# Feed-forwards tied to the written plan: layer 0's whole, layer 1's up to its part-sum products

## The chip, the cores and the metric

The kernel runs on one core of one Trainium2 chip. The metric is the device time of one execution in microseconds (us); for several runs the median is given. A core has TensorE (PE; its weight loads are PEld in the profile), VectorE (DVE), ScalarE (ACT), GpSimd (POOL) and SyncE (SP), whose instruction streams run side by side and wait for each other through semaphores. All bulk transfers of this kernel are issued from SP's queue.

## The reference, cut to what matters

Two layers over 512 latent tokens and 256 context tokens of width 1024, in 32-bit floating point. Each layer is a token mixer (windowed attention in layer 0, differential attention in layer 1) and a feed-forward of width 4096, each followed by a residual and a LayerNorm. Layer 1 needs only the latent tokens.

```python
alpha = DEEPNORM_ALPHA                                   # (2 * DEPTH) ** 0.25
x = layer_norm(alpha * x + g1 * ax, ln1_g[i], ln1_b[i])
fx = sqrelu_mlp(x * (1.0 + sc2) + sh2, mlp_w1[i], mlp_w2[i])
x = layer_norm(alpha * x + g2 * fx, ln2_g[i], ln2_b[i])
...
def sqrelu_mlp(h, w1, w2):
    return jnp.square(jax.nn.relu(h @ w1)) @ w2
```

g1, g2, sc2 and sh2 are vectors over the width that come from a conditioning product; g1 and g2 are called gates below.

## The kernel before, in words

**Products.** Every large product is three matmuls of split operands (`mm3`, L330 to L332): a value is cast to a shorter format (the "h" part, on ACT) and what the cast lost is a second number (the "l" part, a subtraction on DVE). `wsplit` (L305) loads 128 x 1024 of a weight and does that cast (L313) and split (L319). A weight buffer of the pool has three raw tiles and four h/l pairs.

**A feed-forward.** `main0` and `main1` begin with the attention's output product by blocks of 128 tokens (`tok_product`, tile `y_ps`): six blocks in layer 0, four in layer 1. Behind each block stands a chain: `gated_add` (L586) multiplies the product by the gate row (`g_tmp`, L589) and adds it to the block's accumulator `acc`; `stats` takes its statistics (`bn`); `moments` makes mean and 1/deviation (`mv`, `rstd`, the power on POOL); `normalise` (L538) scales the block in place (L540). Then `ln_job` (L544) has TensorE transpose the block (`xn_t`, L555), ACT apply the scale and shift (`fx` or `hx_v`) and cast (`hx0m`, `hx1m`, `hx`), and DVE split. The residual for the second LayerNorm is needed from the same block: `residual` (L685) multiplies `acc` by the first LayerNorm's weight row and adds its bias row; both rows were multiplied by alpha before (`scale_inplace`, L699). In layer 0, `R0.step` runs it and sends the block to `m_spill`.

`mlp_pipe` (L702) computes the first six column tiles of w1 plainly (`plain`, tile `h_ps`) and the other 26 as 13 pairs with seven instead of eight half products (`pair`; the weights' sums are made by `part_sums`, on POOL, ACT and DVE). Between them run pieces of the second product (`y_groups`, tile `y_ps`, collected in `fx`). At the end `last_y` multiplies what was collected by the second gate and adds it to `acc` (`fold`, two POOL operations for each half block, 24 in layer 0), then runs the last products and the chain of the next LayerNorm behind each block (`final`, L956). In layer 0, `pre1` then starts layer 1's first products (`qkv_ps`).

**The order.** The kernel's code contains a planner, `Flow`. Jobs are generators that yield what they wait for; the planner keeps a time `T` for TensorE, gives every DVE (D), ACT (A), POOL (G) and DMA (Q) operation a price (`dve`, `act`, `pool2`: 0.60, 0.50 and 1.25 us for 512 elements a partition; a DMA of 1024 1.45 us and 2 us to land) and a latency (0.2 us, for the end of `normalise` LNLAT = 6.0, for the last block of layer 0 2.5), and so decides in which order the jobs emit their TensorE work. TensorE's queue is in that order. An operation starts in the plan when its engine is free and its dependencies are done; where several could, the one with the lowest number (the order of making). An operation without dependencies may start earlier in the plan than the time at which it was emitted.

The other engines' queues are ordered by the framework's own list scheduler. Where `fl.pin` is "DAG", each DVE, ACT and POOL operation that has a dependency in the plan gets an order edge from the one before it on its engine, so that the queue is as planned; where it is "", no edges are made. Before the change it is "DAG" from layer 0's attention (L1203), "" from layer 0's feed-forward (L1476), "DAG" in layer 1's attention (L1631) and "" in layer 1's feed-forward (L1973). Most planned operations appear in the profile under the lines of their helpers: DVE L267, ACT L270, POOL L273, DMAs L279; a DVE operation that is also tied behind a certain matmul has L678.

## Time and profile before

| what | value |
|---|---|
| median of 3 runs | 1643.1 us (1641.33 to 1644.98) |
| the profiled execution's own time | 1639.2 us |
| its span, first to last instruction | 1637.4 us |
| mean granted clock of TensorE | 0.991 |
| layer 0's feed-forward | about 308 to 892 us |
| layer 1's feed-forward | about 1250 us to the end |

The profile is one execution, taken by the hardware's profiler. Its page gives busy times and shares by engine; a group line gives an operation by source line, engine, tiles and shape, how often it ran, its busy time and the mean time of one in ns, and then the idle time of its engine just before it with what ended that idle time. A wait line reads: engine and line, what it waited for, total us, times, longest us. A timeline row reads: start, length, engine, line, operation, output<-inputs, shape, how many were merged, and in brackets the idle time before it and what ended it. A windows row gives busy time and instructions of an engine in a stretch, then the clock that TensorE was granted (1.00 is full), the DMA share and the rate. What is named as the end of a wait is inferred; "issue" means that the profile shows nothing.

### The profile page before, as it was taken

How to read it: one execution, taken by the hardware profiler on the slowest of the kernel's cores; microseconds unless marked ns; L12 is line 12 of the kernel's file. 1: busy time of each engine (PE TensorE's matmuls, PEld its weight loads, DVE VectorE, ACT ScalarE, POOL GpSimd, SP SyncE). 2: the span in 40 equal slices, each digit the busy share in tenths (PEclk: the TensorE clock that was granted, in tenths of full speed). 3: DMA queues.
4: the chain of work that ended last, by engine and by line, in shares of the span. 5: the costliest groups of instructions: out<-in, count | busy, mean ns of one | idle time of the engine just before them, and what ended most of it. 6: DMA issues, size and time to landing. Idle time of an engine off the chain costs nothing.

```text
span 1637.4 us, 25213 instructions
## 1 busy us (share of the span) xinstructions
PE 1571.6 (96%) x9465; PEld 1377.9 (84%) x9465; DVE 1142.4 (70%) x2201; ACT 791.2 (48%) x1679; POOL 433.7 (26%) x369
## 2 busy tenths in 40 slices
PE   7999999989999999999997999999999799999998
PEld 5887677779888888888986999999987788888896
DVE  4655676589686777967576677777765876566667
ACT  3465665365334334333425555556552745544450
POOL 1344453102111211121183122220100123223363
PEclk9999999999999999999998999999999899999999
DMA  9111551533344444444332222211132333333321
GB/s 372 48 53 34 181 175 44 173 118 129 102 146 163 142 132 139 158 139 148 110 133 91 81 71 71 72 49 40 39 107 100 104 116 103 103 103 103 103 68 62
DMA packets 66435, 181.18 MB, mean 111 GB/s; under 512 B 7368, under 2 KB 13320, under 8 KB 66312
## 3 DMA queue, kind: packets, MB, share of 16 engines
q1 hardware_dynamic: 66312, 179.56, 32.6%
q8 instruction: 74, 1.21, 0.3%
q14 instruction: 49, 0.40, 0.1%
HBM read 168.49 MB, written 11.04 MB: 110 GB/s over the span
## 4 chain that ended last, share of the span: by engine, by line
PE 78%; DVE 9%; ACT 5%; POOL 3%; issue 3%; DMA 2%; SPq 0%; DVEq 0%; ACTq 0%; POOLq 0%
PE y_ps L331 9%; PE y_ps L332 9%; PE y_ps L330 9%; PE h_ps L330 7%; PE h_ps L331 7%; PE h_ps L332 7%; PE qkv_ps L330 3%; PE qkv_ps L331 3%; PE qkv_ps L332 3%; PE s_ps L1785 2%; PE o_ps L1395 2%; PE pT_ps L1413 2%; PE o_ps L1823 2%; POOL acc L273 1%; PE q_ps L330 1%
## 5 line engine op out<-in xcount | busy, mean ns | idle before, releaser
L331 PE MATMUL y_ps<-w_l,hid 128*128 128x512 f32 (+1 forms) x648 | 255.0, 393 | 1.6 <-DVE w_l L319 1.6
L330 PE MATMUL y_ps<-w_h,hid 128*128 128x512 f32 (+1 forms) x648 | 255.7, 395 | 0.6 <-DVE fx L267 0.6
L332 PE MATMUL y_ps<-w_h,hid 128*128 128x512 f32 (+1 forms) x648 | 254.9, 393 | 0.0
L319 DVE TENSOR_TENSOR w_l<-w_raw,w_h 128x1024 fp32r<-128x1024 f32 (+1 forms) x133 | 160.1, 1212 | 47.9 <-ACT w_h L313 46.4
L313 ACT CAST w_h<-w_raw 128x1024 fp32r<-128x1024 f32 (+1 forms) x133 | 131.1, 1002 | 104.8 <-PE y_ps L332 76.7
L332 PEld LDWEIGHTS y_ps<-w_h,hid 128*128 128x128 f32 x648 | 122.2, 189 | 28.6
L331 PEld LDWEIGHTS y_ps<-w_l,hid 128*128 128x128 f32 x648 | 122.3, 189 | 27.5 <-DVE w_l L319 2.9
L267 DVE TENSOR_TENSOR w_half<-w_raw,w_half 128x512 fp32r<-128x512 f32 x130 | 105.8, 824 | 54.7 <-ACT w_half L270 54.3
L330 PEld LDWEIGHTS y_ps<-w_h,hid 128*128 128x128 f32 x648 | 122.4, 189 | 25.4 <-DVE fx L267 1.0
L270 ACT CAST w_half<-w_raw 128x512 fp32r<-128x512 f32 x130 | 79.2, 621 | 128.0 <-PE h_ps L332 97.8
L330 PE MATMUL qkv_ps<-w_h,hx 128*128 128x384 f32 (+1 forms) x384 | 128.6, 335 | 3.2 <-ACT w_h L313 3.2
L273 POOL TENSOR_TENSOR w_sum<-w_raw 128x512 f32<-128x512 f32 x26 | 42.7, 1643 | 328.0 <-DMA w_raw<-in_w 265.1
L331 PE MATMUL qkv_ps<-w_l,hx 128*128 128x384 f32 (+1 forms) x384 | 123.6, 322 | 2.5 <-DVE w_l L319 2.5
L273 POOL TENSOR_TENSOR e<-e,sm 128x512 f32<-128x512 f32 (+2 forms) x96 | 93.5, 990 | 112.7 <-DVE sm L267 77.8
L332 PE MATMUL qkv_ps<-w_h,hx 128*128 128x384 f32 (+1 forms) x384 | 122.9, 320 | 0.0
L267 DVE TENSOR_TENSOR fx<-y_ps,fx 128x512 f32<-128x512 f32 x110 | 75.2, 686 | 36.1 <-PE y_ps L332 35.8
L270 ACT ACTIVATE relu<-relu 128x384 f32<-128x384 f32 (+3 forms) x104 | 69.3, 671 | 61.2 <-DVE relu L267 59.9
L273 POOL TENSOR_TENSOR rope<-rope,rope 128x256 f32<-128x256 f32 (+1 forms) x40 | 35.3, 883 | 216.3 <-DVE rope L267 138.8
L273 POOL TENSOR_TENSOR w_raw<-w_raw,w_sum 128x512 f32<-128x512 f32 x26 | 39.1, 1506 | 197.3 <-DVE w_half L267 160.4
L678 DVE CUSTOM_DVE_ANT_0 w_raw<-w_raw,cB 128x512 f32<-128x512 f32 x112 | 84.0, 784 | 4.7 <-PE y_ps L332 4.1
L270 ACT ACTIVATE e<-e,nm 128x513 f32<-128x513 f32 (+2 forms) x96 | 65.9, 687 | 30.8 <-DVE nm L267 26.8
L330 PEld LDWEIGHTS qkv_ps<-w_h,hx 128*128 128x128 f32 x384 | 72.8, 189 | 5.7 <-ACT w_h L313 3.6
(268 smaller groups left out, 4315.1 us busy)
## 6 DMA issues: line engine op xcount, KB each, us to landing
w_raw<-in_w SPq DMA_DIRECT2D x128, 512.0 KB, 3.6
w_raw<-in_w_adaT SPq DMA_DIRECT2D x56, 512.0 KB, 3.8
w_raw<-in_w_ada SPq DMA_DIRECT2D x24, 512.0 KB, 4.0
w_raw<-in_b_w SPq DMA_DIRECT2D x32, 384.0 KB, 3.9
raw<-in_w_ada SPq DMA_DIRECT2D x16, 512.0 KB, 9.6
w_raw<-in_a_wq SPq DMA_DIRECT2D x8, 512.0 KB, 8.7
w_raw<-in_a_wo SPq DMA_DIRECT2D x8, 512.0 KB, 4.2
w_raw<-in_b_wo SPq DMA_DIRECT2D x8, 512.0 KB, 4.5
```

Source lines behind the costliest of these rows:

```text
L267: return fl.op("D", dve(n), deps, lat, fn(**kw))
L270: return fl.op("A", act(n), deps, lat, fn(**kw))
L273: return fl.op("G", us, deps, lat, fn(**kw))
L313: last["cast"] = nc.scalar.copy(out=h[:, :n], in_=raw[:, :n])
L319: last["split"] = nc.vector.tensor_tensor(**kw)
L330: nc.tensor.matmul(out=o, lhsT=lh, rhs=rh, start=start, stop=False, **kw)
L331: nc.tensor.matmul(out=o, lhsT=lh, rhs=rl, start=False, stop=False, **kw)
L332: last["pe"] = nc.tensor.matmul(out=o, lhsT=ll, rhs=rh, start=False, stop=stop, **kw)
L678: i = fn(**kw)
L1395: nc.tensor.matmul(out=po[odd * HD:odd * HD + HD, 0:256], lhsT=vv[:, kb, kvh], rhs=pt_[:, odd * 256:odd * 256 + 256], start=(i == 0), stop ...
L1413: nc.tensor.transpose(out=pp[:, c * P:(c + 1) * P], in_=es[j][:, i * P:(i + 1) * P], identity=ident)
L1785: nc.tensor.matmul(out=sp[:, c * 512:c * 512 + 384], lhsT=qTt[:, tt, hl, qb * P:(qb + 1) * P], rhs=kS[:, tt, c * 384:c * 384 + 384], start ...
```

## The change

- Both feed-forwards begin with `fl.pin = "DAG"`; the chain of order edges isn't restarted before layer 1's attention. In layer 1 the pin is set to "" after the plain products, where the part sums begin. In layer 0 the pin stays, but from that place on `fl.loose` leaves the casts and splits of weights (in `wsplit` and in `part_sums`) without edges.
- LNLAT goes from 6.0 to 0.2, for the last block of layer 0 too.
- `residual` takes the unscaled rows and multiplies by alpha itself: two `scalar_tensor_tensor` in place of two `tensor_tensor`. The scalings of the rows (two in layer 0, two in layer 1) are gone. In the plan the residual now depends on the rows' transfers and, in layer 0, on TensorE's place.
- `fl.low` adds LOW = 100 to an operation's number: for layer 0's residuals and for the first two tiles of w1.
- `w1` asks for a w1 tile once, one tile ahead; the first two of layer 0 when the fifth block's chain is emitted, the first of layer 1 at the third block's. Layer 0's first three transfers get an order edge behind the last transfer of gate rows and accumulators.
- The final adds depend in the plan on the folds of their half block; `done` gets the statistics of both halves (`flat` resolves such nested lists).

```diff
-LNLAT = 6.0
+LNLAT = 0.2
+LOW = 100
@@ Flow.op
-        t.eng, t.us, t.seq = eng, us, self.n
-        for d in deps:
+        t.eng, t.us, t.seq = eng, us, self.n + LOW * self.low
+        for d in flat(deps):
@@ wsplit
-        a = fl.op("A", act(n), [q, hg], ins=last["cast"])
+        a = fl.op("A", act(n), [q, hg], ins=None if fl.loose else last["cast"])
...
-            d = fl.op("D", dve(n), [a], ins=last["split"])
+            d = fl.op("D", dve(n), [a], ins=None if fl.loose else last["split"])
@@ reload
-        dma(D - c0, [], out=b[:, c0:], in_=src[:, c0:].broadcast_to([P, D - c0]))
+        return dma(D - c0, [fl.pe(0.0)], out=b[:, c0:], in_=src[:, c0:].broadcast_to([P, D - c0]))
@@ residual
-    def residual(acc, g, b, after=None):
-        d = dv(D, [], behind(nc.vector.tensor_tensor, after), out=acc, in0=acc, in1=g, op=ALU.mult)
-        return dv(D, [d], nc.vector.tensor_tensor, out=acc, in0=acc, in1=b, op=ALU.add)
+    def residual(acc, g, b, deps, after=None):
+        d = dv(D, deps, behind(nc.vector.scalar_tensor_tensor, after), out=acc, in0=acc, scalar=ALPHA, in1=g, op0=ALU.mult,
+               op1=ALU.mult)
+        return dv(D, [d], nc.vector.scalar_tensor_tensor, out=acc, in0=b, scalar=ALPHA, in1=acc, op0=ALU.mult, op1=ALU.add)
@@ before mlp_pipe
+    W1 = {}
+
+    def w1(l, ft):
+        if ft < 6 and (l, ft) not in W1:
+            kept = queue["behind"]
+            if l == 0 and ft < 3:
+                queue["behind"] = queue["w1"]
+            W1[l, ft] = wsplit(t["w1"][l, ft])
+            queue["behind"] = kept
+        return W1.get((l, ft))
@@ plain
+                        W[ft] = w1(l, ft)
+                        w1(l, ft + 1)
...
-                        W[ft] = wsplit(t["w1"][l, ft])
@@ last_y, final
-                              half == 1 if l else half == 0 or tb == ntb - 1)
+                              half == 1 if l else half == 0 or tb == ntb - 1, more=[folds[half, tb]])
@@ mlp_pipe, after the plain products
+        if l == 0:
+            fl.loose = True
+        else:
+            fl.pin = ""
         weights(3, 4)
@@ layer 0's feed-forward
-    fl.pin = ""
+    fl.pin = "DAG"
...
+        queue["w1"] = queue["last"]
...
         def done1(tb, st, r):
+            if tb == NTB - 2:
+                fl.low = True
+                w1(0, 0)
+                w1(0, 1)
+                fl.low = False
...
-                d = residual(acc[tb], gx, gc, last["pe"])
+                fl.low = True
+                d = residual(acc[tb], gx, gc, rows + [fl.pe(0.0)], last["pe"])
+                fl.low = False
...
-            for b_, i in ((gx, 0), (gc, 1)):
-                reload(b_, lnrow[0, i:i + 1])
-                scale_inplace(b_, ALPHA)
+            rows[:] = [reload(b_, lnrow[0, i:i + 1]) for b_, i in ((gx, 0), (gc, 1))]
...
-                          LNLAT if tb < NTB - 1 else 2.5), 0)
+                          LNLAT), 0)
@@ layer 1's attention
-        fl.prev, fl.pin = {}, "DAG"
+        fl.loose = False
+        fl.pin = "DAG"
@@ layer 1's feed-forward
-    fl.pin = ""
+    fl.pin = "DAG"
...
-        scale_inplace(lb, ALPHA)
...
         def done3(tb, st, r):
+            if tb == NXB - 2:
+                w1(1, 0)
...
-            reload(gx, lnrow[1, 0:1])
-            scale_inplace(gx, ALPHA)
-            res = [lambda tb=tb: residual(acc[tb], gx, lb, last["pe"]) for tb in range(NXB)]
+            row = reload(gx, lnrow[1, 0:1])
+            res = [lambda tb=tb: residual(acc[tb], gx, lb, [row], last["pe"]) for tb in range(NXB)]
```

More of the change, by code (lines that the diff above doesn't have):

```diff
@@ L60, in __init__, with flat @@
         self.done, self.ins = None, None
+def flat(x):
+    return [z for y in x for z in flat(y)] if isinstance(x, (list, tuple)) else [x]
 class Flow:
@@ L74, in __init__ @@
         self.events = []
-        self.prev, self.order, self.pin = {}, None, ""
+        self.prev, self.order, self.pin, self.loose, self.low = {}, None, "", False, False
     def pe(self, us):
@@ L583, in hxs, with gated_add @@
         return hx[k // 2][:, k % 2, hl, sl]
-    def gated_add(pool, give, acc, half, pt, p, gate, last, scale=1.0):
+    def gated_add(pool, give, acc, half, pt, p, gate, last, scale=1.0, more=()):
         cs_ = slice(half * 512, (half + 1) * 512)
@@ L596, in gated_add @@
                       op0=ALU.mult, op1=ALU.add)
+        m = [m, *more]
         if last:
-            return dv(512, [m], nc.vector.tensor_tensor, out=acc[:, cs_], in0=acc[:, cs_], in1=tm, op=ALU.add)
-        return gp(pool2(512), [m], nc.gpsimd.tensor_tensor, out=acc[:, cs_], in0=acc[:, cs_], in1=tm, op=ALU.add)
+            return dv(512, m, nc.vector.tensor_tensor, out=acc[:, cs_], in0=acc[:, cs_], in1=tm, op=ALU.add)
+        return gp(pool2(512), m, nc.gpsimd.tensor_tensor, out=acc[:, cs_], in0=acc[:, cs_], in1=tm, op=ALU.add)
     def tok_mm(src, W, tb, pt, u):
@@ L752, in half @@
                 w = R.half_tile(nhalf[0] - 1)
-                a = ac(512, [dep, R.rhalf.get()], nc.scalar.copy, out=w[:, 0:512], in_=src)
-                d = dv(512, [a], nc.vector.tensor_tensor, out=w[:, 512:1024], in0=src, in1=f(w)[:, 0:512],
-                       op=ALU.subtract)
+                a = nc.scalar.copy(out=w[:, 0:512], in_=src)
+                a = fl.op("A", act(512), [dep, R.rhalf.get()], ins=None if fl.loose else a)
+                d = nc.vector.tensor_tensor(out=w[:, 512:1024], in0=src, in1=f(w)[:, 0:512], op=ALU.subtract)
+                d = fl.op("D", dve(512), [a], ins=None if fl.loose else d)
                 rel = Task()
@@ L895, in pair @@
             yield from mix(3)
-        gates, st, Wy, fresh = [], {}, {}, set()
+        gates, st, Wy, fresh, folds = [], {}, {}, set(), {}
         def y_weights(c, half, n=2):
@@ L920, in fold @@
             d = gp(pool2(512), [d], nc.gpsimd.tensor_tensor, out=x, in0=x, in1=g[:, cs_], op=ALU.mult)
-            gp(pool2(512), [d], nc.gpsimd.tensor_tensor, out=acc[tb][:, cs_], in0=acc[tb][:, cs_], in1=x, op=ALU.add)
+            folds[half, tb] = gp(pool2(512), [d], nc.gpsimd.tensor_tensor, out=acc[tb][:, cs_], in0=acc[tb][:, cs_], in1=x,
+                                 op=ALU.add)
         def sink(c, half, tb, pt, p, slot):
@@ L957, in final @@
                 r = gated_add(R.pool, lambda x: sm_.give(slot, x), acc[tb], half, pt, p, gates[0 if tb < NXB else 1],
-                              half == 1 if l else half == 0 or tb == ntb - 1)
+                              half == 1 if l else half == 0 or tb == ntb - 1, more=[folds[half, tb]])
                 st[tb], r = stats(acc[tb], half, r, st.get(tb))
-                r_half[tb] = r
+                first_half, r_half[tb] = r_half.get(tb), r
                 if half:
-                    done(tb, st[tb], r)
+                    done(tb, st[tb], [first_half, r])
             early, r_half = [], {}
@@ L1029, in last_y @@
                     sm_.give(slot, m)
-                    r = dv(256, [m], nc.vector.tensor_tensor, out=acc[tb][:, cs_], in0=acc[tb][:, cs_], in1=tm, op=ALU.add)
+                    r = dv(256, [m, folds[1, tb]], nc.vector.tensor_tensor, out=acc[tb][:, cs_], in0=acc[tb][:, cs_], in1=tm,
+                           op=ALU.add)
                     r = dv(256, [r], nc.vector.bn_stats, out=parts[:, n + 1], in_=acc[tb][:, cs_])
@@ L1500, in hybrid_block @@
         acc = [apool_top.tile([P, D], F32, name="acc0", tag="acc", bufs=NTB) for _ in range(NTB)]
+        rows = []
         gx, gc = [bcast_load(pool, gate_d[(0, 2)][s:s + 1], f"g1{s}", 512, 2) for s in range(2)]
```

## The prediction

> **What bounds the kernel now.** I read the page first, then who waited for whom on TensorE in four stretches, then the clock by windows, and last the order of instructions where the waits are long. Busy time and instructions of each engine:
>
> ```profile
> span 1637.4 us, 25213 instructions
> PE 1571.6 (96%) x9465; PEld 1377.9 (84%) x9465; DVE 1142.4 (70%) x2201; ACT 791.2 (48%) x1679; POOL 433.7 (26%) x369
> ```
>
> TensorE is busy for 96% of the span, and the change adds or removes no matmul. It can win only waits of TensorE in the two feed-forwards, and the time in which TensorE works at half clock after them. These are the waits (engine and line, what it waited for, total us, times, longest) around the start of layer 0's feed-forward (340 to 362 us), in its middle (400 to 860), at its end (862 to 900) and at the start of layer 1's (1268 to 1312):
>
> ```profile
> PE xn_t L555 <- issue: 5.2, 1, 5.2
> ...
> PE h_ps L330 <- ACT relu L270: 3.1, 2, 1.6
> PE gate_t L462 <- DVE mods L267: 2.3, 2, 2.0
> PE y_ps L331 <- DVE w_l L319: 1.6, 3, 0.6
> ...
> PE xn_t L555 <- DVE g_tmp L589: 4.9, 3, 2.8
> PE qkv_ps L330 <- ACT w_h L313: 2.9, 1, 2.9
> PE qkv_ps L331 <- DVE w_l L319: 1.4, 1, 1.4
> PE xn_t L555 <- POOL rstd L273: 0.9, 1, 0.9
> ...
> PE h_ps L330 <- ACT relu L270: 3.5, 2, 2.0
> PE h_ps L331 <- DVE hx1m L267: 1.9, 1, 1.9
> PE h_ps L330 <- ACT hx1m L270: 1.6, 1, 1.6
> PE xn_t L555 <- DVE acc L540: 1.2, 1, 1.2
> PE xn_t L555 <- ACT fx L270: 0.5, 1, 0.5
> ```
>
> They add up to 5.2, 7.0, 10.1 and 8.7 us. Next, TensorE alone by windows: the stretch, its length, busy time, instructions, granted clock, DMA share, GB/s.
>
> ```profile
> 356.40:361.10 4.70, 4.63 (x22) 0.50 0.27 112
> ...
> 861.00:868.50 7.50, 7.50 (x33) 1.00 0.17 70
> 868.50:889.70 21.20, 15.40 (x77) 0.92 0.23 87
> ...
> 892.60:900.40 7.80, 6.38 (x22) 0.57 0.47 152
> ...
> 1275.90:1282.70 6.80, 4.55 (x19) 0.50 0.39 140
> ...
> 1296.00:1310.00 14.00, 10.46 (x73) 0.88 0.35 113
> ```
>
> Busy time multiplied by what is missing from full clock gives the price of the slow clock: 4.63 x 0.50 = 2.3 us at the start; 15.40 x 0.08 + 6.38 x 0.43 = 1.2 + 2.7 = 3.9 at the end; 4.55 x 0.50 + 10.46 x 0.12 = 2.3 + 1.3 = 3.6 in layer 1. So the start of layer 0 can give 7.5 us, its end 14.0, layer 1's start 12.3 and the middle 7.0.
>
> **A, start of layer 0's feed-forward.** The first two rows are TensorE's last token product and its transposes of that block; the others are VectorE (DVE) in between.
>
> ```profile
> 345.24 0.39 PE L332 MATMUL y_ps<-w_h,hx 128*128 128x512 f32 x1
> 356.46 0.87 PE L555 MATMUL xn_t<-identr,acc 128*128 128x128 f32 x3 [5.17 <-issue]
> ...
> 347.93 0.69 DVE L589 TENSOR_TENSOR g_tmp<-y_ps,g 128x512 f32<-128x512 f32 x1
> ...
> 349.80 0.68 DVE L267 SCALAR_TENSOR_TENSOR acc<-acc,g_tmp 128x512 f32<-128x512 f32 x1
> 350.40 1.22 DVE L678 TENSOR_TENSOR acc<-acc,g 128x1024 f32<-128x1024 f32 x1
> ...
> 353.61 0.69 DVE L267 TENSOR_SCALAR g<-g 128x1024 f32<-128x1024 f32 x1 [1.06 <-DMA g<-in_lnrow]
> ...
> 355.55 0.81 DVE L540 TENSOR_SCALAR acc<-acc,mv,rstd 128x1024 f32<-128x1024 f32 x1 [0.44 <-POOL rstd L273]
> ```
>
> The product ends at 345.6, yet the last block's normalise ends only at 356.4: its first step starts 2.3 us late, and a residual (1.22), the scaling of a row that first waits for its DMA (1.06 + 0.69) and splits stand inside the chain. The change deletes the scaling, puts the residuals and the first two w1 splits behind (100 added to their number in the plan), and has DVE keep the plan's order. Without strangers the chain is 0.69 + 0.68 and, by the rows in B, 2.61 from the statistics to the end of the normalise, with handoffs some 4.2 us: done by 349.8, before TensorE first needs it at 351.3. The wait and the slow clock behind it go, 7.5 us. What may be late next: the plan counts 1.45 + 2 us for a row from its issue; if the chip's row lands later, the residual stands in DVE's line and waits for it, and behind it the splits of the last two blocks. That costs nothing (the matmuls of the first four blocks come ahead) to 3.5 us (the 1.06 seen, plus two passes of 1.22). I take 1.5, nearer to nothing. **A = -6.0**, bounds -7.5 and -4.
>
> Two residual passes now carry the factor as scalar_tensor_tensor. The 512-wide one above took 0.68, so 1024 take between 1.22 (the pass it replaces) and 1.36: twelve passes cost at most 1.7 us of DVE, against four scalings of 0.69 gone. Zero on the path in between.
>
> The w1 transfers get an order edge behind the loads of the gate rows and accumulators. SP's queue now:
>
> ```profile
> 322.31 0.32 SPq L279 DMA_DIRECT2D acc<-y_spill  x1
> 323.02 1.01 SPq L279 DMA_DIRECT2D w_raw<-in_w  x2
> ```
>
> They already stand right behind the last of these, so the edge costs 0; as w1 is now asked for earlier in the program, without the edge it could go ahead of them. The casts of these first tiles need the buffers of the out-projection's weights, which that product holds to its end, so asking earlier gains 0 too. That the chain of order edges is no longer cut between the stages adds no instruction.
>
> **B, end of layer 0's feed-forward.** POOL and DVE around the folds (the partial results multiplied by the gate and added), then ACT's weight cast:
>
> ```profile
> 795.93 1.81 POOL L273 TENSOR_TENSOR w_raw<-w_raw,w_sum 128x512 f32<-128x512 f32 x1
> 826.10 3.27 POOL L273 TENSOR_TENSOR fx<-fx,g 128x512 f32<-128x512 f32 x2 [28.36 <-DMA g<-gate_d]
> ...
> 855.52 0.67 DVE L589 TENSOR_TENSOR g_tmp<-y_ps,g 128x512 f32<-128x512 f32 x1
> 863.55 0.69 DVE L267 BATCH_NORM_STATS2 bn<-acc 128x6 f32<-128x512 f32 x1 [7.37 <-POOL acc L273]
> ...
> 865.35 0.81 DVE L540 TENSOR_SCALAR acc<-acc,mv,rstd 128x1024 f32<-128x1024 f32 x1 [0.67 <-POOL rstd L273]
> ...
> 891.58 2.41 ACT L313 CAST w_h<-w_raw 128x768 fp32r<-128x768 f32 x3
> ```
>
> In the plan a fold's first product depends on nothing (L985 hands it None), so the plan starts the 24 POOL operations when POOL gets free, about 798, while the chip starts them at 826 when the gate row lands. The plan then sees block 0's normalise some 4.8 us after 855.5 (0.67, POOL's 1.25, 2.61, handoffs), at 860.3; the chip has it at 866.2. Today's 6 us of LNLAT cover just that. With 0.2 the transposes stand behind the next two half blocks: 33 matmuls in 7.5 us make 12 of them 2.7 us, so at 855.5 + 5.4 = 861. TensorE would wait there 5 us, with all later matmuls in its queue behind, and lose 2.3 of clock as in A. Against that, the waits for g_tmp, which stands behind normalises in DVE's line today, end, and the qkv weights no longer wait for ACT: their casts are left loose, LayerNorm work is done sooner, but one cast and one split of 0.95 (cast: 2.41 for three, 0.8 each) still follow the last product, 1.8 us. 14.0 - 5.0 - 2.3 - 1.8 leaves 4.9. **B = -4.9**, bounds -14 (no wait left) and +0.3 (the new wait's 7.3, while qkv's 2.9 + 1.4 + 2.7 stay and 7.0 go).
>
> By the Trainium skill (TensorE: Matmul & The Clock Gate, section What's actually happening) the array falls to half clock after an idle window of about 3.4 us and needs about as long busy to come back. The trace agrees at A (5.2 us idle, then 0.50). By that rule B's new wait costs only about 1.7 of clock, and the sum would be 0.6 lower.
>
> **C, start of layer 1's.** The chain of waits there:
>
> ```profile
> 1270.02 1.31 POOL w_sum L273
> ...
> 1273.29 1.14 DVE w_l L319
> ...
> 1275.02 0.59 DVE g1x L267
> ```
>
> The part sum goes ahead of a LayerNorm's power on POOL, the split and the scaling of a row ahead of its steps on DVE. The pins take the last two out: 1.73. The part sum is not pinned and may stay. If the waits after 1275 shorten by that, the clock loss (2.3) goes too; the relu waits (3.5, and 1.3 of clock) stay. **C = -4.0**, bounds -12.3 and 0.
>
> **D, middle.** Weights float, the rest keeps the plan's order; its waits of 7.0 may shrink or new ones come. The plan prices a 512-wide DVE pass at 0.60 and a POOL one at 1.25; I take +1.0, bounds -7 and +21 (third rival). The flat list helper and the passed-on dependencies issue nothing.
>
> **Sum.** -6.0 - 4.9 - 4.0 + 1.0 = -13.9. The profiled execution took 1639.2 us (span 1637.4, 1.8 around it), so it would take 1625.3; the median of the runs, 1643.1, lies 3.9 higher, and 1643.1 - 13.9 = 1629.2.
>
> **Rivals.** First, only A comes through: B's new wait and the slow clock repeat at the second block, C is DVE's throughput rather than its order, D as taken: -6 + 1 = -5, 1638. For it: plan and chip are 28 us apart at the folds. Second, nothing moves: order edges fix what the list scheduler did anyway and waits go to other instructions, 1643. Against it stand A's strangers. Third, slower: in the middle, DVE and ACT stand in line behind an operation that the plan sees earlier than the chip has it. This row (820 to 900 us) shows such a slip, beside the 0.68 of A:
>
> ```profile
> L267 DVE TENSOR_TENSOR acc<-acc,g_tmp 128x512 f32<-128x512 f32 x7 | 10.5, 1494 | 0.5
> ```
>
> If each of the 13 pairs then pays what the two longest pay now (1.6 for relu), 21 us come, against 14.9 won: 1649. It decides from 14.9 / 13 = 1.15 us a pair. Against it: in a pair nearly everything pinned waits for TensorE itself. The Trainium skill (SBUF — State Buffer, section Who interferes with whom) names why passes stretch: a DVE pass with two SBUF inputs and a GpSimd one that reads SBUF exclude each other; the trace agrees (1494 ns). Fourth, more: A whole, B down to its 1.8, C all but the relu waits, nothing in D: -7.5 - 12.2 - 7.5 = -27.2, 1616.
>
> **How the numbers follow.** Forecast 0.46, first rival 0.19, no move 0.13, slower 0.12, more 0.10. A median of this kernel tells 0.2% (3.3 us) from no change, so 1638 counts as faster three times in four: faster 0.46 + 0.10 + 0.14 = 0.70, same 0.13 + 0.05 = 0.18, slower 0.12. The forecast's own range is 1622 to 1637; with the rivals' ends and half of "more" left out, 1614 to 1646.
>
> **What would show it.** A: the transposes of the last block at 351 without a 5 us wait, no residual row before that normalise, clock 1.00 until 373. B: first xn_t near 861 with a wait of 4 to 6 us; g_tmp no longer the releaser; qkv within 2 us of the last y_ps. C: no g1x and l1b scaling, first h_ps matmul by 1276. D: PE waits between 400 and 860 summing to 5 to 9 us. The forecast is wrong if the middle's sum passes 20, or if the qkv start still waits 4 us.

## The result, and the profile after

| | before | after |
|---|---|---|
| median of 4 runs each | 1642.4 us (1641.3 to 1645.0) | 1628.0 us (1627.9 to 1628.9) |
| profiled execution (span) | 1639.2 us (1637.4) | 1627.9 us (1626.1) |

The ratio is 0.9911, 95% interval 0.9894 to 0.9928: faster by 0.9%, 14.4 us in the medians and by 11.3 in the two profiled executions. The forecast was 1629.2 in a range of 1614 to 1646. The time came out right; much of the working behind it did not, as the experiments show.

From here on, line numbers are those of the changed kernel (`mm3` L335 to L337, cast L318, split L324, `normalise` L545, `xn_t` L560, `g_tmp` L594, first pass of `residual` L684, the line of operations tied behind a certain matmul; DVE's, ACT's and POOL's helpers L272, L275 and L278). The page after, span and engines:

```profile
span 1626.1 us, 25216 instructions
...
PE 1568.7 (96%) x9465; PEld 1374.5 (85%) x9465; DVE 1141.9 (70%) x2197; ACT 790.2 (49%) x1679; POOL 449.9 (28%) x369
```

The work is the same but for four scalings of DVE; POOL's 16 us more are for the most part two passes that took 14.94 and 8.71 us (7, and the last section). What went is idle time of TensorE and matmuls at half clock. TensorE's waits after, in the stretches 400 to 860 us, 850 to 900, 1250 to 1312 and 1312 to 1345 (the stretch 340 to 362 has no row any more):

```profile
PE h_ps L335 <- DVE relu L272: 2.7, 3, 1.5
PE gate_t L467 <- DVE mods L272: 2.0, 1, 2.0
PE y_ps L336 <- DVE w_l L324: 1.8, 3, 0.8
PE y_ps L335 <- ACT w_h L318: 1.8, 2, 1.1
PE y_ps L335 <- DVE fx L272: 1.0, 1, 1.0
PE h_ps L335 <- ACT relu L275: 0.4, 1, 0.4
...
PE xn_t L560 <- DVE acc L545: 4.6, 1, 4.6
PE y_ps L336 <- DVE w_l L324: 0.3, 1, 0.3
PE y_ps L335 <- ACT hx_v L275: 0.3, 1, 0.3
...
PE h_ps L335 <- ACT relu L275: 2.2, 2, 1.5
PE h_ps L336 <- DVE hx1m L272: 1.1, 1, 1.1
PE xn_t L560 <- ACT hx1m L275: 0.7, 1, 0.7
PE h_ps L337 <- DVE w_l L324: 0.5, 1, 0.5
...
PE h_ps L335 <- ACT relu L275: 3.7, 2, 3.0
```

The 5.2 us at the start of layer 0 are gone. By all waits in these same stretches, the end of layer 0 went from 10.6 to 5.2, the start of layer 1 from 8.9 to 4.5 and the middle from 7.8 to 9.7 (the prediction's 10.1, 8.7 and 7.0 lack a few small rows). The last row, behind the start of layer 1, is new. The granted clock after, where it had been low or is now (stretch, length, busy time and matmuls of TensorE, clock, DMA share, GB/s):

```profile
351.00:361.10 10.10, 10.10 (x89) 1.00 0.70 232
861.00:870.70 9.70, 5.14 (x17) 0.65 0.23 93
1264.50:1281.00 16.50, 14.85 (x125) 1.00 0.42 130
1322.00:1328.00 6.00, 3.78 (x16) 0.72 0.49 165
```

The clock is full at both starts and low behind the two waits of 4.6 and 3.0 us.

Where the time went is best read by milestones of TensorE in the timelines. Before, layer 0's first pair begins at 422.6 us, its last `h_ps` ends at 825.8, the last `qkv_ps` at 1204.8, the last matmul of layer 1's attention at 1245.7, layer 1's first pair begins at 1326.7, and the span ends at 1637.4. The table gives, for every kernel of this study, the us gained (-) or lost (+) against that in each stretch of its profiled execution. A is the start of layer 0's feed-forward, D its middle, B its end with the qkv products, C the start of layer 1's.

| kernel | A | D | B | attention | C | rest | sum | median | ratio (95%) |
|---|---|---|---|---|---|---|---|---|---|
| after | -4.6 | +2.7 | -8.0 | +1.5 | -8.5 | +5.6 | -11.3 | 1628.0 | 0.9911 (0.9894 to 0.9928) |
| latency alone, on before | +10.5 | +3.1 | -4.8 | 0.0 | -1.8 | -0.1 | +6.9 | 1647.0 | 1.0022 (1.0008 to 1.0035) |
| after, old latency | +2.8 | +0.9 | -2.7 | 0.0 | -0.5 | +5.5 | +6.2 | 1643.3 | 1.0000 (0.9986 to 1.0013) |
| after, w1 asked late | +22.3 | +3.5 | -8.1 | +1.5 | -1.1 | +5.0 | +23.1 | 1658.3 | 1.0085 (1.0067 to 1.0103) |
| after, no order edges | -0.5 | +1.5 | -6.8 | +1.5 | -4.3 | -0.1 | -8.6 | 1630.3 | 0.9927 (0.9912 to 0.9941) |
| after, edges in layer 0 only | -4.5 | +0.8 | -8.2 | +1.5 | -4.3 | -0.1 | -14.8 | 1625.6 | 0.9900 (0.9884 to 0.9917) |
| after, LOW = 0 | -3.8 | +1.5 | -8.6 | +1.6 | -7.8 | +5.7 | -11.5 | 1626.2 | 0.9899 (0.9882 to 0.9915) |
| after, rows scaled | -2.8 | +2.7 | -8.1 | +1.5 | -7.6 | +5.6 | -8.8 | 1629.7 | 0.9913 (0.9895 to 0.9930) |
| after, old latency at B | -3.9 | +0.6 | -2.9 | 0.0 | -7.9 | +6.0 | -8.1 | 1632.0 | 0.9935 (0.9921 to 0.9950) |
| edges in layer 0, gate row first | -3.1 | +1.2 | -12.9 | 0.0 | -4.9 | -0.1 | -19.8 | 1619.2 | 0.9855 (0.9827 to 0.9883) |
| after, residuals moved | -4.0 | +2.0 | -7.7 | 0.0 | -8.5 | 0.0 | -18.3 | 1622.5 | 0.9871 (0.9838 to 0.9904) |
| after, both remedies | -3.0 | +2.5 | -11.3 | 0.0 | -8.6 | +0.2 | -20.1 | 1619.1 | 0.9845 (0.9827 to 0.9863) |
| after, one-input passes | -4.7 | +1.3 | -8.6 | +1.5 | -7.9 | +3.0 | -15.4 | 1623.8 | one run |

One of the four runs with edges in layer 0 only took 1909.1 us at a mean clock of 0.753 and is not counted here (with it the median is the 1626.1 that an expectation below names).

Equal stages differ between executions: A, in the seven kernels that leave it as in "after", lies between -3.0 and -4.7, D there between +0.6 and +2.7, the attention, which nothing touches, at 0.0 or +1.5. Differences of under 2 us in one stage are therefore not read. Each ratio stands against runs of the kernel before on the same chip; a time of one row is only roughly comparable with a time of another.

### The profile page after: what moved, and what is told of

Same layout as the page of the kernel before. It is cut to its first block, busy times and chain, and to the rows that moved or that the text cites. A ratio compares the mean times of both kernels' runs of the same rounds, so it can differ in the third digit from the quotient of the medians.

```text
span 1626.1 us, 25216 instructions
## 1 busy us (share of the span) xinstructions
PE 1568.7 (96%) x9465; PEld 1374.5 (85%) x9465; DVE 1141.9 (70%) x2197; ACT 790.2 (49%) x1679; POOL 449.9 (28%) x369
## 3 DMA queue, kind: packets, MB, share of 16 engines
q8 instruction: 74, 1.21, 0.3%
## 4 chain that ended last, share of the span: by engine, by line
PE 47%; DVE 7%; POOL 4%; ACT 2%; issue 2%; DMA 1%; SPq 0%; DVEq 0%; POOLq 0%; ACTq 0%
PE y_ps L335 5%; PE y_ps L337 5%; PE y_ps L336 5%; PE h_ps L335 5%; PE h_ps L337 4%; PE h_ps L336 4%; PE qkv_ps L335 3%; PE qkv_ps L336 3%; PE qkv_ps L337 3%; PE s_ps L1819 3%; PE o_ps L1857 2%; POOL acc L278 1%; PE pT_ps L1885 1%; DVE acc L272 1%; POOL w_raw L278 1%
## 5 line engine op out<-in xcount | busy, mean ns | idle before, releaser
L335 PE MATMUL y_ps<-w_h,hid 128*128 128x512 f32 (+1 forms) x648 | 257.1, 397 | 3.0 <-ACT w_h L318 1.8
L337 PE MATMUL y_ps<-w_h,hid 128*128 128x512 f32 (+1 forms) x648 | 256.0, 395 | 0.0
L324 DVE TENSOR_TENSOR w_l<-w_raw,w_h 128x1024 fp32r<-128x1024 f32 (+1 forms) x133 | 160.1, 1212 | 53.6 <-ACT w_h L318 52.1
L318 ACT CAST w_h<-w_raw 128x1024 fp32r<-128x1024 f32 (+1 forms) x133 | 130.9, 1000 | 107.0 <-PE y_ps L337 91.8
L335 PEld LDWEIGHTS y_ps<-w_h,hid 128*128 128x128 f32 x648 | 123.2, 190 | 29.1 <-ACT w_h L318 2.5
L337 PEld LDWEIGHTS y_ps<-w_h,hid 128*128 128x128 f32 x648 | 123.0, 190 | 29.1
L278 POOL TENSOR_TENSOR w_sum<-w_raw 128x512 f32<-128x512 f32 x26 | 45.3, 1740 | 314.3 <-DMA w_raw<-in_w 209.1
L335 PE MATMUL qkv_ps<-w_h,hx 128*128 128x384 f32 (+1 forms) x384 | 127.8, 333 | 0.5 <-ACT w_h L318 0.3
L278 POOL TENSOR_TENSOR e<-e,sm 128x512 f32<-128x512 f32 (+2 forms) x96 | 93.5, 990 | 113.6 <-DVE sm L272 81.3
L337 PE MATMUL qkv_ps<-w_h,hx 128*128 128x384 f32 (+1 forms) x384 | 122.2, 318 | 0.0
L278 POOL TENSOR_TENSOR w_raw<-w_raw,w_sum 128x512 f32<-128x512 f32 x26 | 52.5, 2018 | 186.2 <-DVE w_half L773 168.6
L684 DVE CUSTOM_DVE_ANT_0 w_raw<-w_raw,cB 128x512 f32<-128x512 f32 x112 | 88.5, 818 | 14.4 <-PE y_ps L337 12.4
L275 ACT ACTIVATE relu<-relu 128x768 f32<-128x768 f32 (+3 forms) x104 | 69.5, 671 | 51.2 <-DVE relu L272 50.4
L272 DVE TENSOR_TENSOR fx<-y_ps,fx 128x512 f32<-128x512 f32 x110 | 75.1, 686 | 26.5 <-PE y_ps L337 26.3
L278 POOL TENSOR_TENSOR rope<-rope,rope 128x256 f32<-128x256 f32 (+1 forms) x40 | 35.3, 883 | 206.1 <-DVE rope L272 135.8
L275 ACT ACTIVATE e<-e,nm 128x513 f32<-128x513 f32 (+2 forms) x96 | 65.9, 687 | 31.2 <-DVE nm L272 27.1
L335 PEld LDWEIGHTS qkv_ps<-w_h,hx 128*128 128x128 f32 x384 | 72.2, 188 | 2.9 <-ACT sk L275 1.3
```

What stands on the lines that cost most here:

```text
L272: return fl.op("D", dve(n), deps, lat, fn(**kw))
L275: return fl.op("A", act(n), deps, lat, fn(**kw))
L278: return fl.op("G", us, deps, lat, fn(**kw))
L318: last["cast"] = nc.scalar.copy(out=h[:, :n], in_=raw[:, :n])
L324: last["split"] = nc.vector.tensor_tensor(**kw)
L335: nc.tensor.matmul(out=o, lhsT=lh, rhs=rh, start=start, stop=False, **kw)
```

## The experiments

**1. Which part carries the gain: the order edges?** Both feed-forwards without edges:

```diff
@@ layer 0's feed-forward
-    fl.pin = "DAG"
+    fl.pin = ""
@@ layer 1's feed-forward
-    fl.pin = "DAG"
+    fl.pin = ""
```

> The changed kernel without the order edges in both feed-forwards; the latency of 0.2, the high numbers of residuals and first w1 splits, the residual's two-factor form, the fold dependencies and the w1 queue edge stay. Theory (the gain is the order edges' and the numbers work only through them): without edges the number in the plan moves nothing on the chip, so the strangers ahead of the normalise come back at 350, and the POOL strangers of layer 1: 1637 to 1643. Rival 1 (the gain is the removed row scalings and the changed places of the residuals in the program): 1628 to 1632. Rival 2 (the latency of 0.2 without edges puts the transposes too early in TensorE's order at all three places): slower than before, 1645 to 1655.

1630.3 us, in the range of the rival. At most a few us of the 14 are the edges'; by stages they give 4 at A and 4 at C, of which 5.7 are lost again in the last stretch. Edges in layer 0 alone:

> The changed kernel with the order edges in layer 0's feed-forward only, none in layer 1's. Theory by the trace (up to the first pair of layer 1 the change won 8.5 us there and lost 5.6 again at 1324, behind a POOL pass of 14.9 us): the 8.5 are the pins', the 5.6 come or go with the order of POOL's and DVE's passes after 1302, so 1628 + 3 = 1631 with the loss gone, 1636 with the loss staying. Rival (layer 1's gain is the removed scalings and the earlier w1 transfer, not the edges): 1626 to 1629, with the first h_ps of layer 1 still some 27 us behind the last rms_bc.

1625.6, just under the range of the rival, with stages that neither foresaw: C gives 4.3 instead of 8.5, so half of it is the edges', as half of the theory had it, and the later loss of 5.6 is absent. Layer 1's edges as they stand win nothing.

**2. The residuals' and splits' numbers.** `LOW = 100` to `LOW = 0`:

> The changed kernel with the 100 added to the plan's number of residuals and first w1 splits taken away (0), all else as it is. Theory (A was won by putting these behind the LayerNorm chain of the last block): in the plan the residuals of blocks 0 on and the w1 splits stand ahead of the last normalise where they are ready, so 3 to 5 us of wait and 2.3 of clock come back at 351 to 360, time 1633 to 1636. Rival (in the plan the residual's rows come late anyway, so the order edges alone put the residuals behind the chain): the wait at 351 stays away and the time is 1627 to 1630.

1626.2, no wait at 351, A at -3.8: the rival, 0.8 us under its range. The numbers carry nothing that these runs can tell.

**3. The removed scalings.** Rows scaled in place and `tensor_tensor` residuals as before, with edges:

```diff
-    rows[:] = [reload(b_, lnrow[0, i:i + 1]) for b_, i in ((gx, 0), (gc, 1))]
+    for b_, i in ((gx, 0), (gc, 1)):
+        rows.append(reload(b_, lnrow[0, i:i + 1]))
+        scale_inplace(b_, ALPHA)
...
     row = reload(gx, lnrow[1, 0:1])
+    scale_inplace(gx, ALPHA)
...
```

> The changed kernel with the rows scaled in place and the residuals as two tensor_tensor passes, as before; order edges, numbers, latency and early requests stay. Theory of the prediction (a row's scaling that waits for its transfer stands inside the last LayerNorm chain): with edges DVE keeps the plan's place for the scaling, which the plan starts at once, so a wait for the row of 1 to 4 us comes in DVE's line at the start of layer 0 and one at layer 1, time 1630 to 1635. Rival (the scalings are beside the path): 1626.5 to 1629.

1629.7, between the two ranges; the ratio is 0.9913 against 0.9911, and A (-2.8) and C (-7.6) lie at the edge of the spread of equal stages. The wait for a row that the theory expected in DVE's line comes at neither start. What the scalings cost, up to some 2 us, these runs can't tell from nothing.

**4. The latency.** Before with the latency of 0.2 alone, and after with the old 6 and 2.5:

```diff
-LNLAT = 6.0
+LNLAT = 0.2
...
-                          LNLAT if tb < NTB - 1 else 2.5), 0)
+                          LNLAT), 0)
```

This is the edit of the first run; that of the second is its reverse.

> The kernel before with one part of the change alone: the plan's latency behind a normalise 0.2 instead of 6 (and 2.5 for the last block of layer 0), no order edge added. Theory (of the 11.3 us by spans, the run without order edges still won 8.6, and the latency is what sets where TensorE's order has the transposes): most of the 8.6 is the latency's, 1632 to 1636, with the transposes of layer 1 beginning some 4 us earlier behind the last rms_bc. Rival (the gain without edges is the removed row scalings, the residuals' new places and the earlier w1 transfers): 1640 to 1645.

> The changed kernel with the old latencies (6 us, 2.5 for the last block of layer 0) at all three LayerNorm stages; order edges and all else as changed. Theory (the latency is the larger part, the edges the smaller): 1634 to 1640, the wait at 861 gone, qkv waiting as in the run with the old latency at the end of layer 0 alone, and the start of layer 1 slower by 3 to 5 us. Rival (the edges and the latency are each enough, they overlap): 1630 to 1633, no slower than that run's 1632.

Neither theory held, nor a rival. The latency alone loses 3.7 us (1647.0 against 1643.3), and everything but the latency gains nothing (1643.3, ratio 1.0000). So the latency pays only together with something else of the change, and in the main that isn't the order edges, for without them 1630.3 is reached. TensorE's waits from 316 to 375 us of the kernel with the latency alone:

```profile
PE xn_t L555 <- ACT w_h L313: 8.8, 1, 8.8
PE xn_t L555 <- DMA acc<-y_spill: 5.3, 1, 5.3
```

The timelines of DVE and TensorE there, the last block's normalise and the first plain product:

```profile
362.20 0.81 DVE L540 TENSOR_SCALAR acc<-acc,mv,rstd 128x1024 f32<-128x1024 f32 x1 [0.44 <-POOL rstd L273]
...
364.70 0.56 PE L330 MATMUL h_ps<-hx0m,w_h 128*128 128x256 f32 x1
```

With the short latency all transposes stand ahead of the plain products; before the change the first plain product, at 345.47 us, stood ahead of the transposes of the last two blocks. So TensorE has nothing to do while the last block's chain runs, with splits and the scaling of a row in it. Its transposes begin at 363.11, 0.1 us after the normalise has ended. The profile names ACT's cast as the end of the 8.8 us, but that cast was over at 362.3. The 5.3 us belong to the first block's transposes: without the order edge of the change, three w1 transfers stand ahead of the gate rows and accumulators (5, and A below).

**5. The early request.** That points to the edits around w1, which the prediction costed at nothing. After, with each w1 tile asked for where it was before (with the requests goes the order edge that they carried, so the first three w1 transfers stand ahead of the gate rows again):

```diff
-            if tb == NTB - 2:
-                fl.low = True
-                w1(0, 0)
-                w1(0, 1)
-                fl.low = False
...
-            if tb == NXB - 2:
-                w1(1, 0)
...
-                        W[ft] = w1(l, ft)
-                        w1(l, ft + 1)
+                        W[ft] = wsplit(t["w1"][l, ft])
```

> The changed kernel with w1's tiles asked for where they were before (each in the plain products, when its PSUM tile is taken), all else as changed. Theory (the run with the latency alone waited 8.8 us for the first w_h of layer 0 and 3.0 for a w_l in layer 1, because with the short latency the request stands behind all LayerNorm work; the early request is what lets the latency pay): first h_ps of layer 0 at 353 or later instead of 348, a wait of 4 us or more for w_h or w_l before it, another of 2 us or more at the start of layer 1, time 1633 to 1640. Rival (as the prediction costed it: asking earlier gains nothing, and in the other run it was the missing order edges that let strangers ahead): 1627 to 1630.

1658.3 us: this turns 14 us of gain into 15 of loss, beyond the theory's range and against the rival. TensorE by windows in that kernel:

```profile
340.00:380.00 40.00, 34.31 (x204) 0.87 0.32 106
```

After the change it is busy for all of the 40.00 us there, at full clock; in the next 40 us it is 34.35 at a clock of 0.91 against 38.62 at 1.00.

ACT's timeline, the first cast of a w1 tile, asked for late:

```profile
361.72 1.04 ACT L318 CAST w_h<-w_raw 128x1024 fp32r<-128x1024 f32 x1
```

And asked for early, after the change:

```profile
344.95 1.08 ACT L318 CAST w_h<-w_raw 128x1024 fp32r<-128x1024 f32 x1
```

Early, it is done before TensorE gets to the first plain product (348.2 us). Late, 10 us of TensorE's busy time are missing between 340 and 420, and the clock falls to 0.87.

TensorE's waits tell the parts. It waits 4.6 us at 321 for the first block's normalise, because DVE waits 6.47 us for the gate row, which stands behind w1's transfers (2.78 after the change); that is the order edge's part. It waits 4.2 us until the last block's normalise ends at 359.8, with no plain product ahead of those transposes; then 1.4 for w_h and w_l of the first tile and 5.7 for those of later tiles. So the wait of 4 us for w_h or w_l that the theory expected ahead of the first `h_ps` (362.8) isn't there, as the 8.8 us that it started from were no wait for w_h either (4); the late request costs as much through the order of TensorE's queue. The waits of over 2 us for w_h and w_l at the start of layer 1 came (3.8 and 2.6).

**6. The new wait at the end of layer 0.** The old latency there alone, edges and all else as changed:

```diff
-                          LNLAT), 0)
+                          6.0 if tb < NTB - 1 else 2.5), 0)
```

> The changed kernel with one thing put back: the plan counts 6 us (2.5 for the last block) behind a normalise at the end of layer 0, as before; every order edge stays. Theory (the plan starts the folds some 28 us before the chip does, and the latency had covered that): the 4.6 us wait at the first xn_t near 861 and its 6.8 us half-clock window go, the first qkv matmul comes 4 to 7 us earlier than 886.0, and the time is 1621 to 1625. Rival 1 (the transposes of every block now come later and the qkv product waits for the last ones): the wait moves to the qkv start, 2 to 5 us there, time 1626 to 1631. Rival 2 (the wait comes from POOL's chain and is the same wherever the transposes stand): 4 to 5 us stay near 861 to 868, time 1628.

Rival 1, a little worse than it said: 1632.0. The wait at 861 is gone. TensorE's longest waits from 850 to 900 in that kernel:

```profile
PE qkv_ps L335 <- ACT w_h L318: 3.5, 1, 3.5
PE xn_t L560 <- DVE g_tmp L594: 3.1, 1, 3.1
```

They are much those of before the change. Moving the transposes back doesn't mend the plan's wrong start of the folds. Mending the folds themselves: the first gate row's load goes ahead of the six reloads of the accumulators (here on the kernel with edges in layer 0 alone).

```diff
     def tail(self):
+        need((0, 5))
+        R0.g = [bcast_load(pool, gate_d[(0, 5)][0:1], "g20", 0, 2)]
         p_ = open_top("mlp0c")
...
-    return [bcast_load(pool, gate_d[(0, 5)][s:s + 1], f"g2{s}", 0, 2) for s in range(2)]
+    return R0.g + [bcast_load(pool, gate_d[(0, 5)][1:2], "g21", 0, 2)]
```

> The kernel with order edges in layer 0 alone (1626.1), and there the load of the first gate row put ahead of the six reloads of the accumulators in the transfer queue. Theory (the new wait of 4.6 us at 861 and the 6.8 us at half clock behind it come from the folds, which start when the gate row lands near 826): POOL's first fold product starts before 816, the folds end 4 us or more earlier than 860, the wait at the first xn_t falls below 1 us, 4 to 8 us are won: 1618 to 1622. Rival 1 (the second row's load, which waits for a buffer until 826, or the reloads now standing behind the row, hold the folds as long): the wait stays 4 us or more, 1625 to 1628. Rival 2 (POOL's early folds collide with the part sums and splits of the last pairs): h_ps waits of 2 us or more between 795 and 826, 1626 to 1630.

1619.2, as the theory had it. Its signs came nearly: POOL starts at 817.3, not before 816, and its chain ends 3.7 us earlier, not 4. The timelines of SP's queue and of POOL around the folds after the change (the two loads of gate rows are the row with x2; POOL's first row is the first fold, the next the first block's last addition):

```profile
811.62 3.06 SPq L284 DMA_DIRECT2D acc<-m_spill  x6
814.72 9.56 SPq L284 DMA_DIRECT2D g<-gate_d  x2
...
824.00 2.54 POOL L278 TENSOR_TENSOR fx<-fx,g 128x512 f32<-128x512 f32 x2 [30.89 <-DMA g<-gate_d]
...
860.13 1.28 POOL L278 TENSOR_TENSOR acc<-acc,g_tmp 128x512 f32<-128x512 f32 x1
```

The same with the row first:

```profile
812.05 0.33 SPq L284 DMA_DIRECT2D g<-gate_d  x1
812.42 3.00 SPq L284 DMA_DIRECT2D acc<-m_spill  x6
...
817.27 8.02 POOL L278 TENSOR_TENSOR fx<-fx,g 128x512 f32<-128x512 f32 x4 [24.05 <-DMA g<-gate_d]
...
856.39 1.29 POOL L278 TENSOR_TENSOR acc<-acc,g_tmp 128x512 f32<-128x512 f32 x1
```

And TensorE's wait for the normalise from 850 to 900 us there:

```profile
PE xn_t L560 <- DVE acc L545: 1.6, 2, 0.9
```

One transfer issued 2.7 us earlier starts POOL 6.7 us earlier (5.2 us after its issue instead of 9.3, now that the reloads stand behind it) and ends its chain 3.7 us earlier; the wait falls from 4.6 to 1.6, in two pieces of less than 1 us, and B gains 12.9 instead of 8.2 (the same kernel without it).

**7. The new wait in layer 1.** The timelines after the change: POOL's pass at 1307 us, the end of an unbroken row of DVE's passes, ACT, and TensorE:

```profile
1307.30 14.94 POOL L278 TENSOR_TENSOR w_raw<-w_raw,w_sum 128x512 f32<-128x512 f32 x1 [6.79 <-ACT hx1m L275]
...
1320.44 0.68 DVE L773 TENSOR_TENSOR w_half<-w_raw,w_half 128x512 fp32r<-128x512 f32 x1
...
1322.27 0.62 ACT L771 CAST w_half<-w_raw 128x512 fp32r<-128x512 f32 x1 [8.93 <-POOL w_raw L278]
...
1324.22 0.39 PE L335 MATMUL h_ps<-hx_sum,w_half 128*128 128x256 f32 x1 [3.04 <-ACT relu L275]
```

A part-sum subtraction on POOL that takes 1.3 to 2.3 us elsewhere takes 14.94. ACT's next instruction is the cast of its result; behind that stands the copy of `h_ps` for which TensorE waits. Meanwhile DVE runs passes without a gap until 1321.12 (the end of the 1320.44 row), all with two inputs in SBUF, four of the last five being residual passes. Moving those residuals to later pairs:

```diff
             sm_.give(slot, ac(512, [p], nc.scalar.copy, out=x, in_=pt))
-            if half == 0 and R.res:
-                R.res.pop(0)()
             return
...
         if q == 15:
             R.tail()
+        if R.res:
+            R.res.pop(0)()
```

> The changed kernel with layer 1's four residuals issued one in each of the pairs 3 to 6 instead of with the first four partial results. Theory (the POOL pass of 14.9 us at 1307 is held up by two-input passes of DVE that follow each other without a gap until 1321): without the residuals DVE's row of passes ends near 1316, the POOL pass lasts 8 to 11 us, TensorE's wait of 3.0 us at 1324 and the half clock behind it go, 1622 to 1625. Rival 1 (the POOL pass waits for something else than DVE, for instance a read of ACT): it lasts 14 us or more, 1627 to 1629. Rival 2 (the residuals at their new places stretch the part sums of the pairs 3 to 6): new waits of h_ps between 1325 and 1400, 1627 to 1632.

1622.5, the theory. In that kernel's timelines, the POOL pass and the last of DVE's unbroken row:

```profile
1305.95 10.43 POOL L278 TENSOR_TENSOR w_raw<-w_raw,w_sum 128x512 f32<-128x512 f32 x1 [5.59 <-ACT hx1m L275]
...
1314.55 0.68 DVE L773 TENSOR_TENSOR w_half<-w_raw,w_half 128x512 fp32r<-128x512 f32 x1
```

It ends at 1316.38, 1.15 us behind DVE's 1315.23; after the change it ended at 1322.24, 1.12 behind DVE's 1321.12. The wait has no row any more, and the last stretch loses nothing. Whether it is the second input that matters, or DVE being busy at all:

```diff
+    def stand_in(a, deps, after):
+        for i in range(4):
+            if i % 2 == 0:
+                st = small.tile([P, 2, 6], F32, name="bn", tag="bn", bufs=8)
+            dv(512, deps, behind(nc.vector.bn_stats, after), out=st[:, i % 2, :], in_=a[:, i % 2 * 512:i % 2 * 512 + 512])
-    res = [lambda tb=tb: residual(acc[tb], gx, lb, [row], last["pe"]) for tb in range(NXB)]
+    res = [lambda tb=tb: stand_in(acc[tb], [row], last["pe"]) for tb in range(NXB)]
```

> The changed kernel with the eight residual passes of layer 1 left out and sixteen statistics passes of 512 in their place, each with one SBUF input and about as long (0.68), so that DVE stays busy to 1321 or later; layer 1's residual is not computed. Theory (a DVE pass with two SBUF inputs shuts the POOL pass out, one with a single input does not): the POOL pass that begins at 1307 ends about 1.1 us behind the last two-input pass, near 1317, 9 to 11 us long. Rival (any unbroken row of DVE passes shuts it out): it ends only about 1.1 us behind the last statistics pass, near 1322, 14 us or longer.

The timelines of POOL and DVE in that kernel:

```profile
1305.87 9.83 POOL L278 TENSOR_TENSOR w_raw<-w_raw,w_sum 128x512 f32<-128x512 f32 x1 [6.79 <-ACT hx1m L275]
...
1312.20 2.34 DVE L324 TENSOR_TENSOR w_l<-w_raw,w_h 128x1024 fp32r<-128x1024 f32 x2
1314.47 4.83 DVE L684 BATCH_NORM_STATS2 bn<-acc 128x6 f32<-128x512 f32 x8
```

POOL ends at 1315.70, 1.16 us behind the last two-input pass (1314.54), while DVE goes on without a gap for 4.8 us of one-input passes beside it. That is the theory, which had said 1.1.

**8. Both remedies** (6 and 7, edges in both layers):

> The changed kernel with both remedies: the first gate row's load ahead of the accumulators' reloads, and layer 1's residuals in the pairs 3 to 6. Theory (the two stalls are independent, 500 us apart): the gains add, 1628 - 5.0 (by spans, from the gate row) - 5.5 = 1616 to 1619, without a wait over 1.5 us at 861 and 1324. Rival (the order edges of layer 1 gain nothing once the stall is gone): 1619 to 1621, as the run with the gate row and no edges in layer 1.

1619.1 us, 0.9845 (0.9827 to 0.9863) of the kernel before, ahead of the change's 0.9911, and no wait is left at 1324. That time is the upper end of the theory's range and the lower end of the rival's. The wait at 861 is 2.1 us, over the 1.5 that the theory allowed, and B gains 11.3, not 12.9. That layer 1's edges then pay is not settled: C gives 8.6 against the 4.9 of the kernel with the gate row first and no edges there, with nothing lost later, but the medians are equal (1619.1 and 1619.2), as that execution stood 3 us better ahead of layer 1.

## Why the prediction was right or wrong, step by step

**A, -6.0 forecast, -4.6 measured.** What was to be seen came: no wait at 351, clock 1.00 to 373. DVE's timeline after the change:

```profile
352.59 1.22 DVE L684 SCALAR_TENSOR_TENSOR acc<-acc,g 128x1024 f32<-128x1024 f32 x1
353.72 0.81 DVE L545 TENSOR_SCALAR acc<-acc,mv,rstd 128x1024 f32<-128x1024 f32 x1
```

"No residual before that normalise" is wrong: one residual pass stands there and puts the normalise off by 1 us (POOL's power ends at 352.75). It costs nothing that shows. The normalise ends at 354.5, not 349.8, the transposes come at 355.3, and TensorE has first plain products to do until then. The 7.5 us of wait and slow clock did go. The 1.5 us set against them were for a residual that waits for its row; DVE has no such wait. What took some 3 us back are waits of 0.9 us at 321 and 1.4 at 400, and in this execution the stage began 0.9 us later.

Two steps failed that hardly show in the sum, because the edits that they cost at nothing were made. They are about w1. SP's queue and ACT's casts before the change:

```profile
308.00 1.74 SPq L279 DMA_DIRECT2D w_raw<-in_w  x2
312.59 0.33 SPq L279 DMA_DIRECT2D w_raw<-in_w  x1
312.96 0.90 SPq L279 DMA_DIRECT2D g<-gate_d  x2
...
341.32 3.13 ACT L313 CAST w_h<-w_raw 128x1024 fp32r<-128x1024 f32 x3
```

"The edge costs 0" was read from the two transfers at 323.02, but three others stood ahead of the gate rows, as many as the edge holds back. "Asking earlier gains 0 too" supposed that w1's casts wait until the out-projection has ended, at 345.6, but three had begun by 343.4. Both were costed with the latency as it had been, where the first transposes came late and plain products stood ahead of the last ones. The two kernels with the short latency but without these edits wait 5.3 and 4.6 us for the first block, the others 1.0 at most; and with both taken back, A costs 27 us (22.3 + 4.6). By the rows some 7 of these are the transfers' (the wait of 4.6, and 2.0 of clock behind it) and most of the rest the late request's; the two were not run apart. Credit had gone to the numbers (nothing measurable), the scalings (1.8 at most) and the edges of DVE, ACT and POOL (4.1 in that stage).

**B, -4.9 forecast, -8.0 measured.** The new wait was forecast at 861 with 5 us and came at 861.0 with 4.6; g_tmp is no releaser any more. The clock behind it cost 5.14 x 0.35 = 1.8 us, not the 2.3 taken. That is near the 1.7 which the prediction had worked out by the rule of the Trainium skill (TensorE: Matmul & The Clock Gate, section What's actually happening). In layer 1 the trace is stricter than that rule's idle window of about 3.4 us: the clock fell behind a wait of 3.0 us too (0.72 in 1322 to 1328). The term that was mis-sized is the 1.8 us left over at the start of qkv: it measured 0. By waits and clock, 14.5 - 4.6 - 0.6 - 1.8 = 7.5 of the 8.0 are accounted for (14.5 are the prediction's 14.0 and a wait of 0.5 at 850 to 862). The cause given for the wait, folds that start when the gate row lands, is shown by the run with that row first.

**C, -4.0 forecast, -8.5 measured, 5.6 of it lost again.** Waits fell from 8.9 to 4.5 and the 3.6 of slow clock are gone: 8.0 of the 8.5. The mis-sized term is what was to stay, the relu waits of 3.5 and 1.3 of clock; 2.2 of wait and no slow clock stayed. The removed scaling, a third of the 1.73, was the wrong cause: with the scalings back C still gives 7.6. The old latency takes 8.0 of it away, a late request 7.4, missing edges 4.2, so no one of them is enough. "The part sum is not pinned and may stay" was right about the pin, but the part sum left the chain too: POOL runs it at 1263.1, and its last power, at 1271.1, waits for DVE alone. The loss of 5.6 sits 15 us behind the first pair. The prediction asked only for the start of the stage and had no term for it.

**D, +1.0 forecast, +2.7 measured** in this execution, +0.6 to +2.5 in the six others with the same start and middle of layer 0. The sign was right. Between the milestones only 0.7 of it are waits (7.3 before, 8.0 after); the rest is clock, 397.74 us of busy time instead of 395.92 for the same 1961 matmuls. The 9.7 of waits from 400 to 860, just above the 5 to 9 that were to show it, hold the 1.4 at 400 that belong to A.

**The sum.** By spans -4.6 + 2.7 - 8.0 + 1.5 - 8.5 + 5.6 = -11.3, against -13.9 forecast. B and C gave 3.1 and 4.5 more than forecast, A 1.4 less, D cost 1.7 more, and a late loss of 5.6 and 1.5 in the attention, which some profiled executions have and others not, were missing. So errors of 10.2 and 7.6 us cancelled but for 2.6. That the median moved 14.4 and so met 1629.2 within 1.2 us is partly luck. No rival came true.

## What to carry to other kernels

Edits to a plan don't add: here the short latency alone lost 4 us, everything without it gained nothing, and taking back the early request of w1, with the order edge that it carried, turned -14 into +15. So an edit may be costed at nothing only with the other edits already made. When a wait comes from a plan that believes an operation can start before its data is there, bring the data earlier (one transfer ahead in the queue: 5 us) rather than shift what waits for it (4 us worse). And look 20 us behind a stage that got denser: an engine that now runs without gaps can shut out its neighbour.

## What the hardware showed that was not expected

A part-sum subtraction on POOL (128x512, two SBUF inputs), 1.3 to 2.3 us elsewhere, was held off through a whole unbroken row of two-input DVE passes: 14.94 us after the change, with 17 of them begun after it, and 10.43 and 9.83 in two other kernels, each time ending 1.12 to 1.16 us behind the last such pass, while DVE's passes kept their 0.68 and 1.21 us. One-input statistics passes in the same place did not hold it. The Trainium skill (SBUF — State Buffer, section Summary: rules for kernel authors) says that the two exclude each other and that the second to issue is blocked until the first has finished; the trace agrees on which passes exclude each other, but here the block outlasts not one instruction but a row of them that follow without a gap.

Not every such row holds POOL off to its end, and it is not always POOL that gives way. The timelines of POOL and DVE after the change, in the middle of layer 0:

```profile
384.46 8.71 POOL L278 TENSOR_TENSOR w_sum<-w_raw 128x512 f32<-128x512 f32 x1 [31.72 <-DVE acc L272]
...
392.01 1.98 DVE L272 TENSOR_TENSOR relu<-relu 128x768 f32<-128x768 f32 x1
```

This pass of POOL ended 1.15 us behind a DVE pass that ended at 392.02, although the next one, shown here, followed without a gap; that one took 1.98 us instead of 0.95. And 10 us ahead of the pass at 1307, a DVE pass that began 0.4 us after POOL's stretched (the timelines of POOL and DVE):

```profile
1297.19 1.61 POOL L278 TENSOR_TENSOR w_sum<-w_sum,w_raw 128x512 f32<-128x512 f32 x1 [25.40 <-DMA w_raw<-in_w]
...
1297.56 1.78 DVE L272 TENSOR_TENSOR hid<-relu,hid 128x512 fp32r<-128x512 f32 x1
```

What decides between them stays open; no run here tells it.

The 1.5 us that the attention loses in some of the profiled executions are clock alone. TensorE from the last `qkv_ps` to the end of layer 1's attention after the change:

```profile
1194.86:1237.25 42.39, 39.26 (x203) 0.96 0.44 159
```

And with both remedies:

```profile
1193.03:1233.92 40.89, 37.77 (x203) 1.00 0.47 166
```

The matmuls are the same 203 and the waits the same 3.0 us; the busy time is 1.5 us longer, at 0.96 of the clock, in a stage that no edit touches. Each kernel was profiled once, so that one and the same kernel has this loss in one execution and not in another is not shown.
